# Adding up a routing matrix in DRAM by indirect scatters in place of one-hot products

## The chip, the cores and the metric

The kernel runs on one core of a Trainium2 chip. The time is device microseconds for one execution of the whole program; three runs were taken. A profile is one further execution with the hardware profiler on. Engines are named as in the profile: PE is TensorE's matrix unit, PEld its weight load, DVE VectorE, ACT ScalarE, POOL GpSimd, SP SyncE.

## The reference, cut to what matters

The program is one layer of a decoder on 512 tokens of width 1024: two mixers (a linear recurrence and a sparse attention), their gated sum and output projection, and then a PEER feed-forward layer, of which the change concerns the second half:

```
def peer_ffn(x, w_q, sub_keys, u, v):        # per block of 128 tokens; H = 8 heads, K = 16
    q = (xb @ w_q).reshape(TB, H, 2, 128)
    s = einsum('thpc,phnc->thpn', q, sub_keys)
    s1, i1 = top_k(s[:, :, 0], K);  s2, i2 = top_k(s[:, :, 1], K)
    cand = s1[..., :, None] + s2[..., None, :]       # 256 sums a head
    top_s, pos = top_k(cand, K)
    eidx = i1 * 128 + i2 at pos                      # 128 experts of 16384 for each token
    g = softmax(top_s)
    h = einsum('tkd,td->tk', u[eidx], xb)
    a = gelu(h) * g
    return einsum('tk,tkd->td', a, v[eidx])
```

## The kernel before, in words

The tokens are four blocks of 128. Block 0 is computed as the reference writes it: 128 times a row of `peer_u` is gathered for each of its tokens (`row`, L755: an indirect DMA of 128 rows of 4 KB, issued by POOL) and DVE takes a dot product with it (`u_row`, L761), then 128 times a row of `peer_v` is gathered and DVE adds it in (`v_row`, L768). Blocks 1 to 3 (`NT` = 384 tokens) are computed densely: all 16384 experts are 128 chunks of 128 experts (expert i * 128 + j is row i of chunk j). For a chunk, `u_chunk` (L739) loads 512 KB of `peer_u`, splits it into a high and a low part (ACT, DVE) and makes 24 products of 384 columns, and ACT takes gelu of the sum; `v_parts` (L883) loads 512 KB of `peer_v`, splits it likewise, multiplies the gelu with the chunk's slice of G, and `v_product` (L911) makes 18 products of 512 columns that add up in six PSUM banks until the end. G has, for each expert and token, the sum of the routing weights with which the token chose the expert: nearly all of it is zero.

The work around the change stands in this order, and a scheduler of the framework that knows what each instruction needs may set independent instructions of an engine in another order than the text has:

- Mixers, with sixteen `gate(m)` (L416), each of which stores 256 KB from a tile `t2k` (four buffers, shared with other steps) to `gate_d` through ACT's queue.
- The heads (L789): for each of 8 heads two `query`, two `scores`, some `u_chunk` (`UH`: 3 for heads 0 to 6, 7 for head 7), and `picks` (L670), the two levels of top 16 on DVE, which ends in the head's indices (`e12`, `eidx`, `iw12`). `weigh` (L713) makes the softmax of all heads after the last.
- The G stage (L806): 48 more `u_chunk`, and between them 48 groups of 8 tokens. In `g_group` DVE makes a one-hot matrix for the first index and a weighted one for the second (`oz`, `ow`), PE multiplies the two for each token (16 small products a group), ACT copies the result into `stg`, and 12 times SP stores 2 MB of it into `g_d`. `some_rows(R1)` sets one `u_row` beside each chunk but the last eight.
- The V stage (L948): chunks 76 to 127 have `u_chunk` and the v part together, then chunks 0 to 75 have the v part alone and load their gelu again from `h_d` (192 KB a chunk). Every fourth chunk loads 768 KB of G (`gj`). `R2` = 2.9 and `R3` = 0.95 rows of block 0 go beside a chunk of the one and the other kind.

`LEAD` (76) is the number of chunks whose first product is made ahead of the V stage. A row's DVE instruction is set behind the last weight split traced before it (`issue_after`). A `row` tile has four buffers. The framework puts a wait between instructions that touch the same tile or DRAM tensor.

Of the kernel before, what the change touches and what calls it, by code (L numbers as in the profile page):

```python
# [40 lines left out]
def trunk(ctx, tc, A, out, dbg=None):  # L41
# [44 lines left out]
    ya = [big.tile([P, 4, S], F32R, name="ya" + k) for k in "HL"]  # L86
    gate_d = dram.tile([16, P, S], F32, name="gate_d")
    brow_d = dram.tile([8, 640], F32, name="brow_d")
    bias_d = dram.tile([P, 8, 640], F32, name="bias_d")
# [326 lines left out]
    def gate(m):  # L416
        def evg(ps):
            g = wk.tile([P, S], F32, name="t2k", bufs=4)
            dve.tensor_tensor(g, ps, rb, op=OP.mult)
            act.activation(g, g, AF.Sigmoid)  # L420
            act.dma_start(gate_d[m], g)
        proj_T(GA + m * P, evg)

# [141 lines left out]
    gw0 = late.tile([P, P], F32, name="gw0")  # L565
    iw12 = late.tile([P, 3, 3, P], F32, name="iw12")
    NT = 3 * P
# [60 lines left out]
    act.dma_start(iota, A["iota"][:, :16])  # L628
    tva = rk.tile([P, NB, 8, 16], F32, name="tva", bufs=1)
    io16k = rk.tile([P, 16, 16], F16, name="io16k", bufs=1)  # L630
# [39 lines left out]
    def picks(h, sc2):  # L670
# [9 lines left out]
        for z in range(2):  # L680
# [5 lines left out]
                          v1[:, :, 1, None, 0:8].to_broadcast([P, NB, 15, 8]), op=OP.add)  # L686
        tv = tva[:, :, h, :]
        tp = rk.tile([P, NB, 16], U32, name="tp")
# [20 lines left out]
        dve.scalar_tensor_tensor(eidx[:, hs], e12[:, 0, 0], 128.0, e12[:, 1, 0], op0=OP.mult, op1=OP.add)  # L709
        for z in range(2):  # L710
            act.copy(iw12[:, :, z, hs], e12[:, z, 1:, :])

    def weigh():  # L713

        nm = rk.tile([P, NB, 8, 16], F32, name="nm", bufs=1)
        dve.tensor_tensor(nm, tva, tva[:, :, :, 0:1].to_broadcast([P, NB, 8, 16]), op=OP.subtract)
        act.activation(nm, nm, AF.Exp)
        ws = rk.tile([P, NB, 8], F32, name="ws")
        dve.tensor_reduce(ws, nm, axis=AX.X, op=OP.add)
        dve.reciprocal(ws, ws)  # L720
        for b in range(NB):
            o = gw0 if b == 0 else iw12[:, b - 1, 2, :]
            dve.tensor_tensor(o.rearrange("p (h k) -> p h k", h=8), nm[:, b], ws[:, b, :, None].to_broadcast([P, 8, 16]),
                              op=OP.mult)

# [3 lines left out]


    LEAD, UH, AHEAD = 76, [3] * 7 + [7], 2
    UPRE = sum(UH)
    R0, R1, R2, R3, NOROW = 0, 1, 2.9, 0.95, 8
    TG, QJ = 32, 4
    NG = NT // TG
    g_d = dram.tile([NG, P, P, TG], F32, name="g_d")
    h_d = dram.tile([LEAD, P, NT], F32, name="h_d")
# [51 lines left out]
    for h in range(8):  # L789
# [8 lines left out]
        picks(h, sc2)  # L798
    weigh()
    rks.close()  # L800
# [4 lines left out]
    vt = ctx.enter_context(tc.tile_pool(name="vt", reuse_waits="tile", bufs=2))  # L805
    with ExitStack() as st:  # L806
        gt = st.enter_context(tc.tile_pool(name="gt", reuse_waits="tile", bufs=1))
        gq = st.enter_context(tc.tile_pool(name="gq", reuse_waits="tile", bufs=2))
        gps = st.enter_context(tc.tile_pool(name="gps", reuse_waits="tile", bufs=2, space=PSUM))
        iof = gt.tile([P, P], F32, name="iof")  # L810
        act.dma_start(iof, A["iota"])

        io16 = gt.tile([P, P, 2], F16, name="io16")
        dve.tensor_copy(io16, iof[:, :, None].to_broadcast([P, P, 2]))
        TB = 8

        def g_block(b):

            ps = gps.tile([P, 512], F32, name="ps_g")
            for z in range(3):  # L820
                pe.transpose(ps[:, z * P:(z + 1) * P], iw12[:, b, z, :], ident)

            i12 = gq.tile([P, P // TB, 2, TB], F16, name="i12")
            act.copy(i12.rearrange("p g z t -> p z g t"), ps[:, :2 * P].rearrange("p (z g t) -> p z g t", z=2, t=TB))

            wt = gq.tile([P, P], F32, name="wt")
            act.activation(wt, ps[:, 2 * P:3 * P], AF.Copy, scale=16384.0)
            wp = gq.tile([P, P // TB, 2, TB], F16, name="wp")
            wg = wt.rearrange("p (g t) -> p g t", t=TB)
            act.copy(wp[:, :, 0, :], wg)  # L830
            dve.tensor_tensor(wp[:, :, 1, :], wg, wp[:, :, 0, :], op=OP.subtract)
            return i12, wp

        def g_group(b, state, t0):
            i12, wp = state
            if t0 % TG == 0:
                stgs[0] = gt.tile([P, P, TG], F32, name="stg", bufs=2)
            stg = stgs[0]
            sh = [P, TB, P, 2]

            def pairs(t):
                return t[:, t0 // TB].rearrange("p z (q two) -> p (z q) two", two=2)[:, :, None, :].to_broadcast(sh)

            oz = gq.tile(sh, F16, name="oz")
            dve.tensor_tensor(oz, io16[:, None].to_broadcast(sh), pairs(i12), op=OP.is_equal)
            ow = gq.tile(sh, F16, name="ow")
            dve.tensor_tensor(ow.rearrange("p (z q) i two -> p z (q i two)", z=2),
                              oz[:, TB // 2:].rearrange("p q i two -> p (q i two)")[:, None, :].to_broadcast(
                                  [P, 2, TB * P]), pairs(wp), op=OP.mult)
            for q in range(TB // 4):  # L850
                ps = gps.tile([P, 4, P], F32, name="ps_g")
                for k4 in range(4):
                    k = q * 4 + k4
                    for z in range(2):
                        pe.matmul(ps[:, k4, :], oz[:, k // 2, :, k % 2], ow[:, z * TB // 2 + k // 2, :, k % 2],  # L855
                                  start=(z == 0), stop=(z == 1))
                t4 = t0 % TG + q * 4
                act.copy(stg[:, :, t4:t4 + 4].rearrange("p j t -> p t j"), ps)  # L858

        stgs = [None]  # L860
        work = [(b, t0) for b in range(3) for t0 in range(0, P, TB)]
        state = {}
        done = 0
        for j in range(UPRE, LEAD):
            u_chunk(j, up.tile([P, 512], F32, name="ps_u"))
            for _ in range(len(work) * (j + 1 - UPRE) // (LEAD - UPRE) - done):
                done += 1
                b, t0 = work[done - 1]
                if t0 == 0:
                    state[b] = g_block(b)  # L870
                g_group(b, state[b], t0)
                if (t0 + TB) % TG == 0:
                    sync.dma_start(g_d[b * (P // TG) + t0 // TG], stgs[0])
            some_rows(R1 if j < LEAD - NOROW else 0)
    vs = ctx.enter_context(tc.tile_pool(name="vs", reuse_waits="tile", bufs=3))
# [4 lines left out]

    gq_t = [None]

    def v_parts(j, hgt):  # L883
# [15 lines left out]
        if j % QJ == 0:  # L899
            gq_t[0] = vs.tile([P, NG, QJ, TG], F32, name="gj", bufs=2)  # L900
            act.dma_start(gq_t[0], g_d[:, :, j:j + QJ, :].rearrange("g i j t -> i g j t"))
# [35 lines left out]

    order = list(range(LEAD, P)) + list(range(LEAD))
    vrows = list(range(P))
    ahead = [u_chunk(j, up.tile([P, 512], F32, name="ps_u")) for j in range(LEAD, LEAD + AHEAD)]  # L940
    def last_rows():
# [6 lines left out]
    for q, j in enumerate(order[:-2]):  # L948
        if LEAD + AHEAD + q < P:
            ahead.append(u_chunk(LEAD + AHEAD + q, up.tile([P, 512], F32, name="ps_u")))  # L950
        a, v = v_parts(j, ahead.pop(0) if ahead else None)
# [105 lines left out]
```

## Time and profile before

| | us |
|---|---|
| three runs: median, lowest, highest | 1711.28, 1708.59, 1711.89 |
| the profiled execution, its own time | 1711.65 |
| span of its trace, first to last instruction | 1709.9 |
| busy in the span: PE, PEld, DVE, ACT, POOL | 1675.5, 1465.9, 1340.8, 729.3, 377.0 |

A busy PE is no PE at its peak, since matmuls overlap: what one costs is the distance between the starts of two, not the length of one. Of a queue of DMA transfers the engine that issues them is busy only for the issue; a POOL instruction `DMA_INDIRECT` is the issue of an indirect transfer.

### The profile page before, as it was taken

How to read it: one execution, taken by the hardware profiler on the slowest of the kernel's cores; microseconds unless marked ns; L12 is line 12 of the kernel's file. 1: busy time of each engine (PE TensorE's matmuls, PEld its weight loads, DVE VectorE, ACT ScalarE, POOL GpSimd, SP SyncE). 2: the span in 40 equal slices, each digit the busy share in tenths (PEclk: the TensorE clock that was granted, in tenths of full speed). 3: DMA queues.
4: the chain of work that ended last, by engine and by line, in shares of the span. 5: the costliest groups of instructions: out<-in, count | busy, mean ns of one | idle time of the engine just before them, and what ended most of it. 6: DMA issues, size and time to landing. Idle time of an engine off the chain costs nothing.

```text
span 1709.9 us, 24687 instructions
## 1 busy us (share of the span) xinstructions
PE 1675.5 (98%) x9095; PEld 1465.9 (86%) x9097; DVE 1340.8 (78%) x2573; ACT 729.3 (43%) x1052; POOL 377.0 (22%) x284
## 2 busy tenths in 40 slices
PE   8999999999999999999999999999999999999997
PEld 6988887777798888999999999999999978888886
DVE  4776887547699999998988588878887888877785
ACT  4322226734443434566666433333333333333333
POOL 2000000000010000232322144444444442333320
PEclk9999999999999999999999999999999999999999
DMA  7321233127454334798988899999999999999983
GB/s 234 131 81 50 75 125 116 56 94 241 163 177 128 126 123 131 248 359 316 359 316 336 278 338 335 337 331 319 322 317 344 324 336 353 357 333 346 321 299 131
DMA packets 172472, 414.90 MB, mean 243 GB/s; under 512 B 14744, under 2 KB 85784, under 8 KB 170688
## 3 DMA queue, kind: packets, MB, share of 16 engines
q10 hardware_dynamic: 101072, 141.70, 24.4%
q1 hardware_dynamic: 34416, 137.40, 22.6%
q0 software_dynamic: 36864, 134.23, 22.4%
q8 instruction: 71, 1.16, 0.3%
q14 instruction: 49, 0.40, 0.1%
HBM read 366.86 MB, written 49.04 MB: 243 GB/s over the span
## 4 chain that ended last, share of the span: by engine, by line
PE 41%; issue 33%; DMA 11%; POOL 9%; DVE 5%; ACT 1%; POOLq 0%; SPq 0%; ACTq 0%; DVEq 0%
POOL row L757 8%; PE acc L79 6%; PE acc L77 6%; PE acc L78 6%; DMA row<-in_peer_u,eidx 5%; PE ps_mm L77 5%; PE ps_mm L79 5%; PE ps_mm L78 5%; DMA row<-in_peer_v,eidx 4%; PE ps_hg L379 2%; PE ps_hg L77 1%; PE ps_yb L460 1%; PE ps_hg L78 1%; PE ps_hg L79 1%; DMA v_raw<-in_peer_v 1%
## 5 line engine op out<-in xcount | busy, mean ns | idle before, releaser
L108 ACT CAST w_hi<-w_raw 128x1024 fp32r<-128x1024 f32 (+2 forms) x215 | 219.2, 1020 | 401.0 <-PE ps_u L78 125.4
L110 DVE TENSOR_TENSOR w_lo<-w_raw,w_hi 128x1024 fp32r<-128x1024 f32 (+2 forms) x215 | 254.9, 1185 | 84.4 <-ACT w_hi L108 72.1
L757 POOL DMA_INDIRECT row<-in_peer_u,eidx x128 | 178.5, 1394 | 553.6 <-DVE hh L762 503.6
L77 PE MATMUL ps_u<-xfH,w_hi 128*128 128x384 f32 x800 | 274.0, 343 | 1.4 <-ACT hg L744 1.4
L78 PE MATMUL ps_u<-xfL,w_hi 128*128 128x384 f32 x800 | 270.6, 338 | 0.0
L79 PE MATMUL ps_u<-xfH,w_lo 128*128 128x384 f32 x800 | 269.9, 337 | 0.0
L757 POOL DMA_INDIRECT row<-in_peer_v,eidx x128 | 178.6, 1395 | 275.5 <-DVE acc L772 253.3
L78 PE MATMUL acc<-v_lo,aH 128*128 128x512 f32 x540 | 211.2, 391 | 3.3 <-DVE v_lo L895 3.3
L77 PE MATMUL acc<-v_hi,aH 128*128 128x512 f32 x540 | 212.1, 393 | 1.4 <-ACT aH L906 1.1
L79 PE MATMUL acc<-v_hi,aL 128*128 128x512 f32 x540 | 212.1, 393 | 0.1
L906 ACT CAST aH<-aj 128x384 fp32r<-128x384 f32 x128 | 65.6, 513 | 308.7 <-DVE aj L903 138.1
L772 DVE SCALAR_TENSOR_TENSOR acc<-row,ah,acc 128x1024 f32<-128x1024 f32 x127 | 162.6, 1281 | 21.4 <-DMA row<-in_peer_v,eidx 20.7
L762 DVE CUSTOM_DVE_ANT_0 scr<-row,xf 128x1024 f32<-128x1024 f32 x128 | 156.3, 1221 | 20.1 <-DMA row<-in_peer_u,eidx 19.3
L77 PEld LDWEIGHTS ps_u<-xfH,w_hi 128*128 128x128 f32 x800 | 150.2, 188 | 3.5 <-ACT hg L744 1.7
L78 PEld LDWEIGHTS ps_u<-xfL,w_hi 128*128 128x128 f32 x800 | 150.5, 188 | 2.2
L79 PEld LDWEIGHTS ps_u<-xfH,w_lo 128*128 128x128 f32 x800 | 150.2, 188 | 0.0
L895 DVE TENSOR_TENSOR v_lo<-v_raw,v_hi 128x1024 fp32r<-128x1024 f32 x90 | 110.0, 1223 | 24.1 <-ACT v_hi L894 23.5
L78 PEld LDWEIGHTS acc<-v_lo,aH 128*128 128x128 f32 x540 | 101.7, 188 | 24.0 <-DVE v_lo L895 3.6
L79 PEld LDWEIGHTS acc<-v_hi,aL 128*128 128x128 f32 x540 | 101.8, 188 | 23.2 <-DVE aL L908 0.8
L77 PEld LDWEIGHTS acc<-v_hi,aH 128*128 128x128 f32 x540 | 101.7, 188 | 22.1 <-ACT aH L906 1.4
L894 ACT CAST v_hi<-v_raw 128x1024 fp32r<-128x1024 f32 x90 | 94.4, 1048 | 51.6 <-PE acc L79 19.9
L858 ACT COPY stg<-ps_g 128x512 f32<-128x512 f32 x96 | 99.6, 1158 | 3.3 <-PE ps_g L855 3.3
(313 smaller groups left out, 3367.4 us busy)
## 6 DMA issues: line engine op xcount, KB each, us to landing
w_raw<-in_uT SPq DMA_DIRECT2D x128, 512.0 KB
v_raw<-in_peer_v ACTq DMA_DIRECT2D x90, 512.0 KB
g_d<-stg SPq DMA_DIRECT2D x12, 2048.0 KB
gj<-g_d ACTq DMA_DIRECT2D x32, 768.0 KB
w_raw<-in_peer_v ACTq DMA_DIRECT2D x38, 512.0 KB
w_raw<-in_wT SPq DMA_DIRECT2D x31, 512.0 KB
h_d<-hg ACTq DMA_DIRECT2D x76, 192.0 KB
hgr<-h_d ACTq DMA_DIRECT2D x76, 192.0 KB
```

The lines of the kernel that those rows point to most:

```text
L77: pe.matmul(ps, lh, rh, start=first, stop=False, **kw)
L78: pe.matmul(ps, lh, rl, start=False, stop=False, **kw)
L79: pe.matmul(ps, ll, rh, start=False, stop=last, **kw)
L108: act.copy(hi[:, :n], raw[:, :n])
L110: pace[0] = dve.tensor_tensor(lo[:, :n], raw[:, :n], hi[:, :n].bitcast(F32), op=OP.subtract)
L757: pool.indirect_dma_start(out=g, out_offset=None, in_=A[tab], in_offset=bass.IndirectOffsetOnAxis(ap=eidx[:, k:k + 1], axis=0))
L762: dve.tensor_tensor_reduce(out=scr, in0=row("peer_u", k), in1=xf0, scale=1.0, scalar=0.0, op0=OP.mult, op1=OP.add, accum_out=hh[:, k:k + 1])
L772: dve.scalar_tensor_tensor(acc, row("peer_v", k), ah[:, k:k + 1], acc, op0=OP.mult, op1=OP.add)
L858: act.copy(stg[:, :, t4:t4 + 4].rearrange("p j t -> p t j"), ps)
L894: act.copy(vh, raw)
L895: pace[0] = dve.tensor_tensor(vl, raw, vh.bitcast(F32), op=OP.subtract)
L906: act.copy(aH, gj)
```

## The change

G is one DRAM tensor for each block (`g_d[0..2]`, 16384 experts by 128 tokens, 8 MB each). Beside gates 0 to 5 ACT's queue fills them with zeros (12 transfers of 2 MB). `picks` makes, for each head, the softmax weights at once (in place of `weigh`) and the address of each weight (`gi`, expert * 128 + token), and then issues 48 indirect scatters through POOL: for each k of 16 and each block of 3, 128 weights (one a partition, 4 bytes) are added to the words of `g_d[b]` that `gi` names. `gi` and `wh`, which a scatter reads, have three buffers, one a head. The one-hot stage goes. `LEAD` is 96: 32 chunks in the heads (4 a head), 64 between the heads and the V stage, 32 in the V stage with both parts, 96 with the v part alone. Rows of block 0 go beside them at rates 0, 0.7, 2.7 and 1.4. The G of four chunks is loaded one group ahead, as three transfers of 256 KB.

```
+    g_d = [dram.tile([P * P, P], F32, name="g_d%d" % b) for b in range(3)]
+    nil = consts.tile([P, 512], F32, name="nil")
+    pool.memset(nil, 0.0)
...
             act.dma_start(gate_d[m], g)
+            if m < 6:
+                for z in range(2):
+                    act.dma_start(g_d[m // 2][(m % 2 * 2 + z) * 32 * P:(m % 2 * 2 + z + 1) * 32 * P, :].rearrange(
+                        "(p r q) t -> p r (q t)", p=P, q=4), nil[:, None, :].to_broadcast([P, 8, 512]))
...
-        for z in range(2):
-            act.copy(iw12[:, :, z, hs], e12[:, z, 1:, :])
-    def weigh():
...
+        ef = rk.tile([P, 3, 16], F32, name="ef")
+        dve.scalar_tensor_tensor(ef, e12[:, 0, 1:], 128.0, e12[:, 1, 1:], op0=OP.mult, op1=OP.add)
+        gi = rk.tile([P, 3, 16], I32, name="gi", bufs=3)
+        dve.tensor_scalar(gi, ef, 128.0, pcol, op0=OP.mult, op1=OP.add)
+        nm = rk.tile([P, NB, 16], F32, name="nm")
+        dve.tensor_tensor(nm, tv, tv[:, :, 0:1].to_broadcast([P, NB, 16]), op=OP.subtract)
         act.activation(nm, nm, AF.Exp)
+        ws = rk.tile([P, NB], F32, name="ws")
         dve.tensor_reduce(ws, nm, axis=AX.X, op=OP.add)
         dve.reciprocal(ws, ws)
+        wh = rk.tile([P, 3, 16], F32, name="wh", bufs=3)
+        dve.tensor_tensor(wh, nm[:, 1:], ws[:, 1:, None].to_broadcast([P, 3, 16]), op=OP.mult)
+        dve.tensor_scalar(gw0[:, hs], nm[:, 0], ws[:, 0:1], None, op0=OP.mult)
+        for k in range(16):
+            for b in range(3):
+                pool.indirect_dma_start(out=g_d[b].rearrange("e (t one) -> (e t) one", one=1),
+                                        out_offset=bass.IndirectOffsetOnAxis(ap=gi[:, b, k:k + 1], axis=0),
+                                        in_=wh[:, b, k:k + 1], in_offset=None, compute_op=OP.add)
...
-    LEAD, UH, AHEAD = 76, [3] * 7 + [7], 2
+    LEAD, UH, AHEAD = 96, [4] * 8, 2
-    R0, R1, R2, R3, NOROW = 0, 1, 2.9, 0.95, 8
+    R0, R1, R2, R3 = 0, 0.7, 2.7, 1.4
...
-    with ExitStack() as st:
...
+    for j in range(UPRE, LEAD):
+        u_chunk(j, up.tile([P, 512], F32, name="ps_u"))
+        some_rows(R1)
...
+    def g_load(q):
+        if q < P and q % QJ == 0:
+            gqs[q] = vs.tile([P, 3, QJ, P], F32, name="gj", bufs=2)
+            for b in range(3):
+                act.dma_start(gqs[q][:, b], g_d[b].rearrange("(i j) t -> i j t", j=P)[:, order[q]:order[q] + QJ, :])
...
-        dve.scalar_tensor_tensor(gj.rearrange("p (g t) -> p g t", t=TG), gq_t[0][:, :, j % QJ, :], 1.0 / 16384,
-                                 hgt.rearrange("p (g t) -> p g t", t=TG), op0=OP.mult, op1=OP.mult)
+        dve.tensor_tensor(gj.rearrange("p (b t) -> p b t", b=3), gq_t[0][:, :, j % QJ, :],
+                          hgt.rearrange("p (b t) -> p b t", b=3), op=OP.mult)
```

## Rows read from the trace of the kernel before

**Rows 1.** Busy time by stage (heads, G stage, V stage both parts, v alone).

```profile
core 0: us, PE busy (x) PEld busy (x) DVE busy (x) ACT busy (x) POOL busy (x), PEclk, DMA share, GB/s
460.00:691.00 231.00, 224.12 (x1221) 203.06 (x1219) 215.59 (x941) 97.27 (x143) 5.04 (x6) 1.00 0.42 136
691.00:955.00 264.00, 261.05 (x1988) 252.84 (x1989) 220.85 (x238) 170.55 (x207) 71.05 (x45) 1.00 0.88 322
963.00:1374.00 411.00, 410.19 (x2057) 372.56 (x2058) 333.51 (x424) 144.60 (x199) 188.47 (x140) 1.00 0.93 327
1374.00:1690.00 316.00, 312.40 (x1349) 253.90 (x1348) 251.36 (x308) 113.12 (x157) 93.64 (x69) 0.99 0.94 325
```

**Rows 2.** PE in order of time: a u chunk's products, then a v chunk's.

```profile
472.37 0.34 PE L79 MATMUL ps_hg<-xfH,w_lo 128*128 128x384 f32 x1
472.55 0.34 PE L77 MATMUL ps_hg<-xfH,w_hi 128*128 128x384 f32 x1
...
1600.64 0.39 PE L79 MATMUL acc<-w_hi,aL 128*128 128x512 f32 x1
1600.87 0.39 PE L77 MATMUL acc<-w_hi,aH 128*128 128x512 f32 x1
```

**Rows 3.** Gelus of u chunks (L744) counted in the G stage.

```profile
700.00:950.00 250.00, 22.81 (x48) 1.00 0.88 323
```

**Rows 4.** Costliest groups by line: mean ns of one, idle before, releaser.

```profile
L757 POOL DMA_INDIRECT row<-in_peer_v,eidx x128 | 178.6, 1395 | 275.5 <-DVE acc L772 253.3 <-issue 10.3 <-DVE hh L762 5.6
L858 ACT COPY stg<-ps_g 128x512 f32<-128x512 f32 x96 | 99.6, 1158 | 3.3 <-PE ps_g L855 3.3
L845 DVE TENSOR_TENSOR oz<-io,i 128x2048 f16<-128x2048 f16 x48 | 58.5, 1219 | 0.0
L855 PE MATMUL ps_g<-ow,oz 128*128 128x128 f16 x768 | 52.8, 219 | 2.4 <-ACT stg L858 2.4
```

**Rows 5.** POOL in order of time: start, length, gap before it.

```profile
502.34 0.94 POOL L757 DMA_INDIRECT row<-in_peer_u,eidx  x1 [0.30 <-issue]
503.59 0.94 POOL L757 DMA_INDIRECT row<-in_peer_u,eidx  x1 [0.30 <-issue]
...
1119.38 1.34 POOL L757 DMA_INDIRECT row<-in_peer_u,eidx  x1 [0.30 <-issue]
1121.02 1.31 POOL L757 DMA_INDIRECT row<-in_peer_u,eidx  x1 [0.30 <-issue]
...
1127.64 1.71 POOL L757 DMA_INDIRECT row<-in_peer_u,eidx  x1 [0.30 <-issue]
```

**Rows 6.** Index writes of the 8 heads on DVE (L709).

```profile
L709 DVE SCALAR_TENSOR_TENSOR eidx<-e x8: 166/174/175, 498.2 to 688.1; 128x16 int32<-128x16 f32 x8
```

**Rows 7.** A store to DRAM (L203), and a transfer that reads it (L205).

```profile
L203 ACTq DMA_DIRECT2D brow_d<-brow x1: 522/522/522, 25.7 to 25.7; - x1
...
L205 ACTq DMA_DIRECT2D bias_d<-brow_d x1: 564/564/564, 28.2 to 28.2; - x1
```

**Rows 8.** The chain that ended last, 990 to 1020 us: start, length.

```profile
997.06 8.22 DMA row<-in_peer_u,eidx
```

**Rows 9.** Loads of G (L901) and the product that takes one (L903).

```profile
L901 ACTq DMA_DIRECT2D gj<-g_d x32: 367/384/659, 955.2 to 1669.9; - x32
...
L903 DVE SCALAR_TENSOR_TENSOR aj<-gj,hg x52: 548/552/559, 962.7 to 1374.2; 128x384 f32<-128x384 f32 x52
```

**Rows 10.** Gates 0 to 5, then the rest: ACT busy (x), clock, DMA share, GB/s.

```profile
195.00:250.00 55.00, 3.81 (x6) 1.00 0.26 86
250.00:327.00 77.00, 16.58 (x18) 1.00 0.35 112
```

**Rows 11.** The stretch with most DMA, columns as in rows 1.

```profile
1400.00:1500.00 100.00, 99.92 (x434) 81.17 (x433) 85.07 (x104) 37.95 (x52) 30.47 (x25) 1.00 1.01 356
```

More of the change, by code (lines that the diff above doesn't have):

```diff
@@ L565, in trunk @@
     gw0 = late.tile([P, P], F32, name="gw0")
-    iw12 = late.tile([P, 3, 3, P], F32, name="iw12")
+    pcol = late.tile([P, 1], F32, name="pcol")
     NT = 3 * P
@@ L628, in trunk @@
     act.dma_start(iota, A["iota"][:, :16])
-    tva = rk.tile([P, NB, 8, 16], F32, name="tva", bufs=1)
+    act.dma_start(pcol, bass.AP(tensor=A["iota"].tensor, offset=A["iota"].offset, ap=[[1, P], [1, 1]]))
     io16k = rk.tile([P, 16, 16], F16, name="io16k", bufs=1)
@@ L686, in picks @@
                           v1[:, :, 1, None, 0:8].to_broadcast([P, NB, 15, 8]), op=OP.add)
-        tv = tva[:, :, h, :]
+        tv = rk.tile([P, NB, 16], F32, name="tv")
         tp = rk.tile([P, NB, 16], U32, name="tp")
@@ L709, in picks @@
         dve.scalar_tensor_tensor(eidx[:, hs], e12[:, 0, 0], 128.0, e12[:, 1, 0], op0=OP.mult, op1=OP.add)
-        for z in range(2):
-            act.copy(iw12[:, :, z, hs], e12[:, z, 1:, :])
-    def weigh():
-        nm = rk.tile([P, NB, 8, 16], F32, name="nm", bufs=1)
-        dve.tensor_tensor(nm, tva, tva[:, :, :, 0:1].to_broadcast([P, NB, 8, 16]), op=OP.subtract)
+        ef = rk.tile([P, 3, 16], F32, name="ef")
[4 more added lines that the diff above has]
+        dve.tensor_tensor(nm, tv, tv[:, :, 0:1].to_broadcast([P, NB, 16]), op=OP.subtract)
         act.activation(nm, nm, AF.Exp)
-        ws = rk.tile([P, NB, 8], F32, name="ws")
+        ws = rk.tile([P, NB], F32, name="ws")
         dve.tensor_reduce(ws, nm, axis=AX.X, op=OP.add)
         dve.reciprocal(ws, ws)
[L721 to L724, printed above, removed]
-    LEAD, UH, AHEAD = 76, [3] * 7 + [7], 2
+        wh = rk.tile([P, 3, 16], F32, name="wh", bufs=3)
[7 more added lines that the diff above has]
+    LEAD, UH, AHEAD = 96, [4] * 8, 2
     UPRE = sum(UH)
-    R0, R1, R2, R3, NOROW = 0, 1, 2.9, 0.95, 8
-    TG, QJ = 32, 4
-    NG = NT // TG
-    g_d = dram.tile([NG, P, P, TG], F32, name="g_d")
+    R0, R1, R2, R3 = 0, 0.7, 2.7, 1.4
+    QJ = 4
     h_d = dram.tile([LEAD, P, NT], F32, name="h_d")
@@ L798, in trunk @@
         picks(h, sc2)
-    weigh()
     rks.close()
@@ L805, in trunk @@
     vt = ctx.enter_context(tc.tile_pool(name="vt", reuse_waits="tile", bufs=2))
-    with ExitStack() as st:
[L807 to L874, printed above, removed]
@@ L879, in trunk @@
     v3 = A["peer_v"].rearrange("(i j) d -> i j d", j=P)
-    gq_t = [None]
+    order = list(range(LEAD, P)) + list(range(LEAD))
+    gqs, gq_t = {}, [None]
+    def g_load(q):
[3 more added lines that the diff above has]
+                act.dma_start(gqs[q][:, b], g_d[b].rearrange("(i j) t -> i j t", j=P)[:, order[q]:order[q] + QJ, :])
     def v_parts(j, hgt):
@@ L898, in v_parts @@
             act.dma_start(hgt, h_d[j])
-        if j % QJ == 0:
-            gq_t[0] = vs.tile([P, NG, QJ, TG], F32, name="gj", bufs=2)
-            act.dma_start(gq_t[0], g_d[:, :, j:j + QJ, :].rearrange("g i j t -> i g j t"))
         gj = vs.tile([P, NT], F32, name="aj")
-        dve.scalar_tensor_tensor(gj.rearrange("p (g t) -> p g t", t=TG), gq_t[0][:, :, j % QJ, :], 1.0 / 16384,
-                                 hgt.rearrange("p (g t) -> p g t", t=TG), op0=OP.mult, op1=OP.mult)
+        dve.tensor_tensor(gj.rearrange("p (b t) -> p b t", b=3), gq_t[0][:, :, j % QJ, :],
+                          hgt.rearrange("p (b t) -> p b t", b=3), op=OP.mult)
         aH = vs.tile([P, NT], F32R, name="aH")
@@ L936, in finish, with take @@
             q.dma_start(out[b * P:(b + 1) * P, n * 512:(n + 1) * 512], g[:, n, :])
-    order = list(range(LEAD, P)) + list(range(LEAD))
     vrows = list(range(P))
+    g_load(0)
+    def take(q):
+        if q % QJ == 0:
+            gq_t[0] = gqs.pop(q)
+            g_load(q + QJ)
+        return order[q]
     ahead = [u_chunk(j, up.tile([P, 512], F32, name="ps_u")) for j in range(LEAD, LEAD + AHEAD)]
@@ L950, in trunk @@
             ahead.append(u_chunk(LEAD + AHEAD + q, up.tile([P, 512], F32, name="ps_u")))
+        take(q)
         a, v = v_parts(j, ahead.pop(0) if ahead else None)
```

## The prediction

> **What bounds the kernel now.** I read the time by stage first: in every stage PE is busy for all but a few us, at a granted clock of 0.99 to 1.00, with DVE below it and DMA at a share of 0.42 in the heads but 0.88 to 0.94 after them [rows 1]. Since matmuls overlap, I priced them by the distance of two starts in PE's order of time: 0.176 us for 384 columns and 0.23 us for 512 [rows 2]. A u chunk is then 24 × 0.176 = 4.2 us, a v chunk 18 × 0.23 = 4.1 us, both together 8.3 us. The G stage runs 48 chunks in 250 us [rows 3], 5.2 us a chunk: forming G costs PE 1.0 us a chunk, 47 us in all. PE bounds every stage, but DMA is close: at its busiest it moved 356 GB/s at a share of 1.01 [rows 11].
>
> **What goes.** With the one-hot groups go 47 us of PE, and on DVE and ACT work that did not bound: 48 × 2 DVE instructions of about 1.22 us and 96 ACT copies of 1.16 us [rows 4]. The u chunks that change place keep their price, so with nothing late the span would be 1709.9 − 47 = 1663 us. The first v product now comes some 8 us after the first load of G is issued [rows 9], at about 963 us; with 20 more u chunks ahead of it and no G products PE would be ready for it at 963 − 47 + 20 × 4.2 = 1000 us. From it to the end are 1663 − 1000 = 663 us of PE.
>
> **What the heads get.** Four u chunks instead of three a head is 4.2 us more PE beside 1.2 us for the weight split on DVE and seven small DVE instructions in place of `weigh`. DVE is at 216 of 231 us there and PE at 224 [rows 1], so PE, which gets more, stays the bound, and this is in the count above.
>
> **The scatters.** 384 indirect transfers all go through POOL, which has almost nothing to do in the heads. No scatter stands in this trace; the nearest row is the gather, which also takes 128 addresses. Its issue takes 0.94 us and the next starts 0.30 us later when DVE does not disturb it, so at least 1.24 us each; back to back in the V stage it takes 1.31, 1.34 and 1.71 [rows 5], and the mean of all rows of `peer_v` is 1.395 [rows 4], 1.70 with the gap. DVE is less busy with large two-operand work between the heads and the V stage than there. I take 1.45 us, and keep 1.24 and 1.70 for the range (a scatter that is cheaper than a gather is a rival below).
>
> Head 0 has its indices at 498.2 us [rows 6]; with the weights behind them the first scatter can start at about 502. A head makes 48 × 1.45 = 70 us of scatters, but a head lasts only (231 + 4 × 4.2) / 8 = 31 us [rows 1], so POOL falls behind at once and never waits for work again. The last scatter ends at 502 + 384 × 1.45 = 1059 us (978 at 1.24, 1155 at 1.70).
>
> Do their waits add to that? Each scatter writes the tensor that the third scatter before it wrote, so it waits for that one to land. The nearest wait on a store to DRAM is 2.5 us from the store's issue to that of the transfer which reads it, at light load [rows 7]; three issues are 3 × 1.45 = 4.35 us, so the wait is covered. Under load a gather takes 8.2 us from issue to landing, most of it 512 KB of data and other traffic [rows 8]; were a scatter to take that, the wait would bound. I take it as covered, nearer to the small store, and make the other a rival.
>
> *A page on that wait.* The Trainium skill, "DMA: Bandwidth & Descriptors", section "Rules for kernel authors", says that an accumulating transfer reads its destination and writes it later, that another write in between is lost, and that one has to wait for the earlier one's semaphore. No row here shows this.
>
> **Who waits.** `g_load(0)` reads all three tensors, so no v product starts before the last scatter has landed: 1059 + 8 = 1067 us, 67 us after PE could. Behind the scatters on POOL stand the row gathers; DVE's `u_row` waits for them, and behind `u_row` stand the weight splits that PE waits for. `gi` and `wh` have three buffers, so head 7's must wait until head 4's scatters have landed, at 502 + 5 × 70 = 852 us, and DVE, which runs in order, can stand there with splits behind it. Both stalls fall before the V stage and into the same 67 us: the chain on POOL sets the end either way.
>
> **The V stage as a transfer problem.** PE needs 663 us for it. The bytes: u 30 × 0.524 MB, v 128 × 0.524, G 25.2, gelus 96 × 0.197, output 2.1, which is 129 MB; rows 256 × 0.524 = 134 MB if POOL had no time for them earlier. 263 MB at 356 GB/s are 739 us. If 45 rows get between the scatters, the V stage has 239.5 MB, 673 us, but POOL ends 45 × 1.45 = 65 us later: 739 + 1067 = 1806 against 673 + 1132 = 1805. So 1806 both ways. If DMA can give 397 GB/s, the stage is 663 us (this end goes into the range); G's load in runs of 2 KB instead of 512 bytes may help a little.
>
> **The zeros.** 25.2 MB go out on ACT's queue in the 55 us of gates 0 to 5, where 86 GB/s are used [rows 10]: at 356 − 86 = 270 GB/s 14.9 MB fit, and the other 10.3 MB, at 356 − 112 = 244, last 42 us longer. Weights come on SP's queue and have share to spare, but `gate_d`'s stores stand behind the zeros on ACT's queue, and each holds one of four `t2k` buffers, which later gates and `select` need. Between nothing and 42 us, I take 15, and since it comes before head 0 it moves everything: 1806 + 15 = 1821 us of span. What lies around the span is 1711.65 − 1709.9 = 1.75 us, and the profiled execution stood 0.4 us above the median, so 1821 + 1.75 − 0.4: about 1822 us.
>
> **The rivals.**
>
> *Scatters keep up.* POOL's issue of a scatter is much cheaper than that of a gather, so the last lands before 1000 us. Then PE sets the pace: 1663 + 0 to 15 = 1663 to 1678; with the transfers' 673 us in the V stage up to 1690. For it: a scatter moves 4 bytes, not 4 KB, per address. Against: a gather's 0.94 us is POOL's own time, in which no data moves. It decides where the V stage's start and the transfers give back the 47 us: with 739 us of V stage below (1711 − 739 − 8 − 15 − 502) / 384 = 1.16 us a scatter, with 663 us below 1.36 us. That is the span of the doubt: a rate near 1.24 with a DMA near 397 GB/s would also land here, at 978 + 8 + 15 + 663 = 1664, or 1678 with PE's 1000.
>
> The Trainium skill speaks for this rival: "DMA: Bandwidth & Descriptors", section "Anatomy of one DMA — SWDGE (gpsimd) path", puts the fixed 2.0 us of a DMA from this path mostly down to the receipt of the write and calls making descriptors small. By that, three chains of 128 would take 128 × 2.0 = 256 us, an estimate from that page, and the scatters would be free. The gathers' rows disagree on the issue: 0.94 us and more of POOL each [rows 5].
>
> *Each scatter waits for a landing.* Under load a round of three takes 6 us, between the 2.5 us of the small store and the 8.2 us of the gather [rows 7, 8]: 502 + 128 × 6 = 1270, + 8 + 15 + 739 = 2032 us. It decides when a landing takes longer than 4.35 us. For it: the share of DMA is 0.88 and more after the heads now. Against: between heads and V stage there is 512 + 192 KB a chunk of 4.2 us, and a row now and then, far from full.
>
> *It does nothing measurable.* Late scatters cost just the 47 us that PE gains; within 0.2%, which is about what a measurement of this kernel can tell from no change.
>
> **The numbers.** The forecast, POOL's issue as the bound, has 0.60, and by its own bounds goes from 978 + 8 + 739 = 1725 to 1155 + 8 + 739 + 42 = 1944 us. Scatters keep up: 0.20 (1663 to 1707). Landing bound: 0.15 (about 2032, from 1900 up). Nothing measurable: 0.05. So faster 0.20, the same 0.05, slower 0.75. The range has to leave out 2 in 10: I take 1680 to 1940, which cuts half of the keep-up case and most of the landing case, 0.10 each.
>
> **What would show it.** Right: POOL is busy without a gap from about 505 until past 1050 us, PE has a hole of some 50 to 100 us ahead of its first v product, DVE's waits ahead of `u_row` or `gi` name POOL or DMA, DMA is at 350 GB/s or more for most of the V stage, and v chunks alone come every 4.6 us or so instead of 4.1. Wrong: the first v product at about 1000 us with PE unbroken (keep-up), or gaps on POOL of over 1 us between scatters that name a DMA (landing bound). For the zeros: idle time in 200 to 320 us that names `gate_d`. What would make the number wrong most easily is the price of one scatter: 0.1 us is 38 us at the end.

## The result, and the profile after

The changed kernel takes 2141.09 us (median of 4 runs, 2139.67 to 2145.05) against 1710.01 us before (4 runs, 1708.59 to 1711.89): 1.2517 times as long, 95% interval 1.2488 to 1.2546. Slower was forecast, but with 1822 us; the time is 319 us above that and outside the range.

Busy time in stretches of the kernel after; the first two are the stretches of the heads and of the G stage in [rows 1], the third ends as the last scatter is issued, and the last two are the V stage, with both parts and with the v part alone:

```profile
core 0: us, PE busy (x) PEld busy (x) DVE busy (x) ACT busy (x) POOL busy (x), PEclk, DMA share, GB/s
460.00:691.00 231.00, 178.83 (x954) 161.00 (x952) 147.93 (x622) 84.06 (x112) 151.97 (x94) 0.90 0.48 110
691.00:955.00 264.00, 92.83 (x472) 85.55 (x472) 83.82 (x371) 44.48 (x57) 221.44 (x138) 0.69 0.35 47
...
1200.00:1300.00 100.00, 42.16 (x186) 40.55 (x185) 12.99 (x16) 8.62 (x12) 83.54 (x55) 0.70 0.50 97
...
1440.00:1694.00 254.00, 254.00 (x1282) 231.70 (x1281) 198.56 (x285) 91.55 (x125) 114.12 (x78) 1.00 0.89 310
1694.00:2139.00 445.00, 414.82 (x1761) 331.91 (x1759) 368.37 (x441) 151.95 (x211) 172.71 (x128) 0.98 0.92 342
```

Where PE was busy for 261 of 264 us before [rows 1] it is busy for 93 now, and POOL for 221. PE's granted clock is 0.69 there, a mean between its two levels; it is back at 1.00 as the V stage begins. The page draws the same in 40 slices of 53 us, in tenths: POOL's plateau runs from about 510 to 1300 us, and PE's hole lies inside it, from about 640 us, where DVE first stands long at `wh`, until the last scatter.

```profile
PE   8999999999982606225555636999999999999987
...
POOL 1000000003888888888888883123445454454330
PEclk9999999999996858567877867999999999999999
```

What POOL does in the plateau, by line and then in order of time; these answer to the gathers of [rows 4, 5]:

```profile
L737 POOL DMA_INDIRECT g_d<-wh,gi x384 | 634.4, 1652 | 119.6 <-issue 114.6 <-DMA g_d<-wh,gi 4.9
```

```profile
999.74 2.01 POOL L737 DMA_INDIRECT g_d<-wh,gi  x1 [0.30 <-issue]
1002.05 1.56 POOL L737 DMA_INDIRECT g_d<-wh,gi  x1 [0.30 <-issue]
1003.91 2.05 POOL L737 DMA_INDIRECT g_d<-wh,gi  x1 [0.30 <-issue]
```

The issue of a scatter takes 1.65 us in the mean, not the 0.94 of an undisturbed gather or the 1.395 that those of `peer_v` took in the mean [rows 4], and with the gap 1.65 + 119.6 / 384 = 1.96 us. The gap is the same 0.30 us. Waits for a landing are 4.9 us in all 384, so the landing is covered.

First and last start of the scatters, of G's loads (answering to [rows 9]), of the zeros, of the first kind of v product and of `aH`, each from the view of one tile's instructions:

```profile
L737 POOL DMA_INDIRECT g_d<-wh,gi x384: 1552/1558/2597, 514.0 to 1300.3; - x192
L834 ACTq DMA_DIRECT2D gj<-g_d x96: 325/443/1385, 1298.4 to 2085.6; - x96
L429 ACTq DMA_DIRECT2D g_d<-nil x12: 520/521/699, 22.1 to 141.8; - x12
...
L77 PE MATMUL acc<-v_hi,aH x480: 387/389/632, 1446.9 to 2125.7; 128*128 128x512 f32 x160
...
L856 ACT CAST aH<-aj x128: 502/514/520, 1440.6 to 2117.5; 128x384 fp32r<-128x384 f32 x128
```

The V stage (counted from the first `aH` at 1441 us, 140 us after the last scatter) takes 699 us. Why it didn't start at 1302 + 8 = 1310 us is in the waits (us in total, times, longest):

```profile
DVE wh L732 <- DMA g_d<-wh,gi: 259.3, 5, 62.8
DVE scr L774 <- DMA row<-in_peer_u,eidx: 208.1, 26, 16.7
...
PE ps_hg L79 <- DVE w_lo L114: 179.4, 4, 58.8
PE ps_u L79 <- DVE w_lo L114: 179.0, 22, 61.1
...
ACT hg L756 <- DMA g_d<-wh,gi: 60.6, 1, 60.6
...
DVE aj L853 <- DMA hgr<-h_d: 54.0, 36, 3.5
```

DVE stands 259 us for a buffer of `wh`, in five of the eight heads, since the scatters of an earlier head have not read it yet, and 208 us for rows, which POOL gathers between scatters. The weight splits behind these in DVE's order come late, and PE waits for them, 358 us in the heads and after. So when the last scatter lands, 34 u chunks are still to do, at 4.2 us each 143 us.

### The profile page after: what moved, and what is told of

Read it like the earlier page. It is cut to its first block, busy times and chain, and to the rows that moved or that the text cites. A ratio compares the mean times of both kernels' runs of the same rounds, so it can differ in the third digit from the quotient of the medians.

```text
span 2139.5 us, 23585 instructions
## 1 busy us (share of the span) xinstructions
PE 1680.3 (79%) x8320; PEld 1461.0 (68%) x8320; DVE 1234.0 (58%) x2522; ACT 652.2 (30%) x952; POOL 995.4 (47%) x669
## 3 DMA queue, kind: packets, MB, share of 16 engines
q0 software_dynamic: 92160, 134.46, 25.6%
## 4 chain that ended last, share of the span: by engine, by line
PE 34%; POOL 30%; issue 13%; DMA 13%; DVE 7%; ACT 2%; ACTq 1%; SPq 0%; POOLq 0%; DVEq 0%
POOL g_d L737 27%; DMA hgr<-h_d 4%; PE ps_mm L77 4%; PE ps_mm L79 4%; PE ps_mm L78 4%; PE acc L79 4%; PE acc L78 4%; PE acc L77 4%; DMA w_raw<-in_peer_v 3%; DMA g_d<-wh,gi 2%; PE ps_u L79 2%; PE ps_u L77 2%; PE ps_u L78 2%; POOL row L769 2%; DMA v_raw<-in_peer_v 2%
## 5 line engine op out<-in xcount | busy, mean ns | idle before, releaser
L737 POOL DMA_INDIRECT g_d<-wh,gi x384 | 634.4, 1652 | 119.6 <-issue 114.6
L79 PE MATMUL ps_u<-xfH,w_lo 128*128 128x384 f32 x768 | 275.2, 358 | 179.0 <-DVE w_lo L114 179.0
L769 POOL DMA_INDIRECT row<-in_peer_u,eidx x128 | 165.2, 1290 | 291.2 <-DVE hh L774 228.1
L79 PE MATMUL ps_hg<-xfH,w_lo 128*128 128x384 f32 x256 | 89.4, 349 | 179.4 <-DVE w_lo L114 179.4
L79 PE MATMUL acc<-v_hi,aL 128*128 128x512 f32 x480 | 189.0, 394 | 2.0 <-DVE aL L858 1.8
L78 PE MATMUL acc<-v_lo,aH 128*128 128x512 f32 x480 | 188.0, 392 | 2.8 <-DVE v_lo L848 2.8
L77 PE MATMUL acc<-v_hi,aH 128*128 128x512 f32 x480 | 188.1, 392 | 0.0
L71 POOL TENSOR_TENSOR rs_r<-rs_ms,half 128x1 f32<-128x1 f32 (+1 forms) x13 | 11.2, 864 | 357.8 <-DVE rs_ms L69 357.8
L79 PEld LDWEIGHTS ps_hg<-xfH,w_lo 128*128 128x128 f32 x256 | 50.1, 196 | 180.7 <-DVE w_lo L114 180.7
L79 PE MATMUL acc<-w_hi,aL 128*128 128x512 f32 x288 | 115.6, 401 | 10.8 <-DVE aL L858 10.8
```

The source lines that it names most:

```text
L71: pool.tensor_tensor(r, ms, half[:, :k], op=OP.pow)
L77: pe.matmul(ps, lh, rh, start=first, stop=False, **kw)
L78: pe.matmul(ps, lh, rl, start=False, stop=False, **kw)
L79: pe.matmul(ps, ll, rh, start=False, stop=last, **kw)
L737: pool.indirect_dma_start(out=g_d[b].rearrange("e (t one) -> (e t) one", one=1), out_offset=bass.IndirectOffsetOnAxis(ap=gi[:, b, k:k + 1] ...
L769: pool.indirect_dma_start(out=g, out_offset=None, in_=A[tab], in_offset=bass.IndirectOffsetOnAxis(ap=eidx[:, k:k + 1], axis=0))
```

## The experiments

Each is one run beside one of the kernel before on the same chip, which took 1703 to 1714 us; the last two have 6 and 12 runs, beside 17 of the kernel before. Single runs carry no interval, so no reading below rests on a difference of a few us. V start is the start of the first `aH`.

**Eight buffers for the scatters' operands**, so that no head waits for an earlier head's scatters.

```
-        gi = rk.tile([P, 3, 16], I32, name="gi", bufs=3)
+        gi = rk.tile([P, 3, 16], I32, name="gi", bufs=8)
-        wh = rk.tile([P, 3, 16], F32, name="wh", bufs=3)
+        wh = rk.tile([P, 3, 16], F32, name="wh", bufs=8)
```

> gi and wh get eight buffers each, one for every head, so no DVE instruction has to wait for a scatter; nothing else changes. Theory 'price and buffers' (a scatter holds POOL for 1.65 + 0.30 = 1.95 us, and the waits of wh for scatters, 259 us on DVE, kept PE from its u chunks): the first v product comes some 8 us after the last scatter, at about 1310 us instead of 1441, and the time falls by about 130 us to 2010. Rival 'rows take over' (u_row's gathers stand behind the scatters on POOL, and DVE then stands at u_row in place of wh): the time stays within 30 us of 2141 and DVE's waits for gathered rows grow from 208 us to 400 or more.

2140.04 us, V start at 1436: no gain. The heads are done by 740 us, but then DVE meets `u_row`, whose gather stands behind the scatters. The wait and a stretch of this run:

```profile
DVE scr L774 <- DMA row<-in_peer_u,eidx: 451.5, 26, 251.9
```

```profile
800.00:1000.00 200.00, 0.00 (x0) 0.00 (x0) 0.00 (x0) 0.00 (x0) 167.34 (x108) 0.50 0.23 0
```

The 208 us of waits for rows became 452; for 200 us nothing but POOL runs, with PE's granted clock at its lower level. The rows took over from the buffers.

**The rows out of the way as well**: none between the heads and the V stage, more in it.

```
 (gi and wh as above)
-    R0, R1, R2, R3 = 0, 0.7, 2.7, 1.4
+    R0, R1, R2, R3 = 0, 0, 4, 1.45
```

> Eight buffers as in the run before it, and no row of block 0 is set beside the u chunks ahead of the V stage (rates 0, 0, 4 and 1.45 in place of 0, 0.7, 2.7 and 1.4). Price and buffers: POOL has 384 scatters alone, the last ends at about 514 + 384 x 1.95 = 1263 us; the V stage then has all 256 rows, 263 MB, 711 to 739 us: 1980 to 2010 us, like the run before it. Rows take over: this run is 100 us or more faster than the run before it, since only here DVE has nothing left to stand at.

2191.41 us, which neither expected, and V start at 1437 again. DVE no longer stands for `wh`, its waits for rows have fallen to 70 us, and a third gate shows, here in the waits and in ACT's order of time:

```profile
ACT hg L756 <- DMA g_d<-wh,gi: 406.3, 1, 406.3
```

```profile
872.39 0.33 ACTq L758 DMA_DIRECT2D h_d<-hg  x1
1274.58 3.96 ACTq L834 DMA_DIRECT2D gj<-g_d  x3
1278.64 0.49 ACT L756 ACTIVATE hg<-ps_u 128x384 f32<-128x384 f32 x1 [406.29 <-DMA g_d<-wh,gi]
```

The first load of G is issued by ACT, at a place in its order at which 39 of the 98 u chunks ahead of the V stage are still to come, and waits there for the last scatter; all of ACT's gelus and splits wait behind it. In the changed kernel the same wait shows as 61 us, since ACT came to that place only at 1242 us, held up by what DVE owed it. This run is 51 us longer than the one before because its V stage, with all late rows, takes 752 us.

**That load issued by POOL**, which at that place has nothing but scatters ahead.

```
 (as the run before)
-                act.dma_start(gqs[q][:, b], g_d[b]...
+                (pool if q < 8 else act).dma_start(gqs[q][:, b], g_d[b]...
```

> As the second experiment (eight buffers for gi and wh, the row gathers late), and the first two loads of G are issued by POOL instead of ACT. Theory (three in-order queues hold work behind a scatter: DVE at gi and wh, DVE at u_row, ACT at the load of G; with none of them left, POOL alone sets the start of the V stage): ACT has no wait of more than 20 us ahead of a gelu, the 96 u chunks and the two ahead are done by about 1040 us as in the run without scatters, the last scatter comes at about 1275 us as before, the first aH at 1275 + 8 = 1283 us instead of 1437, and with 700 to 750 us of V stage the time is 1985 to 2040 us instead of 2191. Rival (the V stage starts at 1437 because of something else that the last scatter releases, and the three gates are only where it shows): the first aH stays near 1437 us and the time near 2190 us.

2043.87 us, just past the end of what was expected. 97 of the 98 gelus are out before the last scatter, which ends at 1295; V start follows at 1301. What waits now is a v part, for G itself (first the start of `aH`, from the view of its line):

```profile
L856 ACT CAST aH<-aj x128: 503/513/519, 1301.3 to 2022.8; 128x384 fp32r<-128x384 f32 x128
...
DVE aj L853 <- DMA gj<-g_d: 265.8, 1, 265.8
```

Undoing the three gates is worth 97 us: the V stage starts 139 us earlier, but has nearly all rows to take and lasts 741 us, 42 more.

**No scatters** (G stays zero: blocks 1 to 3 get no routed output).

```
-        for k in range(16):
+        for k in range(0):
```

> No scatter is issued (G stays zero: the sum over the experts of blocks 1 to 3 is left out of the result); zeros, weights, addresses, loads of G and all products stay. The prediction's count of the rest: the span before less 47 us of PE, plus 11 us that the zeros cost ahead of the heads, and a V stage between 663 us (PE) and 699 us (as measured after): 1675 to 1712 us. If the V stage is still at 699 us here, with 45 rows set before it, it is the transfers of the 96 v chunks alone that cost the 36 us; if it is at 663, they came from rows that the scatters had pushed into it.

1716.35 us, a little over the 1675 to 1712 expected, where the kernel before took 1702.57 on that chip. V start is at 1012 us, against a forecast of 1000 plus the zeros. The V stage takes 703 us though the rows come on time, in two stretches (both parts, then v alone):

```profile
1012.00:1264.00 252.00, 252.00 (x1271) 229.80 (x1270) 196.52 (x281) 90.46 (x125) 114.23 (x78) 1.00 0.88 310
1264.00:1714.00 450.00, 419.87 (x1763) 335.12 (x1762) 370.66 (x443) 152.26 (x211) 174.84 (x129) 0.97 0.92 339
```

PE needs 96 × 4.14 = 397 us for the 96 v chunks alone and gets through them in 450, of which some 9 follow the last product. So with this `LEAD` and these row rates, scatters that cost nothing would not have beaten the kernel before.

**No scatters, and 76 chunks ahead as before** (with the row rates of before; G zero again).

```
-    LEAD, UH, AHEAD = 96, [4] * 8, 2
+    LEAD, UH, AHEAD = 76, [3] * 7 + [7], 2
-    R0, R1, R2, R3 = 0, 0.7, 2.7, 1.4
+    R0, R1, R2, R3 = 0, 1, 2.9, 0.95
```

> No scatter is issued, so G stays zero and blocks 1 to 3 get no routed output; and 76 chunks have their first product ahead, with the row rates of the kernel before, instead of 96. Theory (in the run without scatters the V stage takes 40 us more than PE needs because the 20 more spilled gelus and the rows bring it to the limit of the transfers): the first aH at about 1012 - 20 x 4.2 = 928 us, the V stage is bound by PE at about 747 us, and the time is 1675 to 1690 us, below the kernel before. Rival (the V stage's rate is set by something else, such as the new load of G): 1705 to 1725 us, as in the run with 96 chunks.

1662.65 us, better than either expected: 51 us below the kernel before, zeros included. The stretch with both parts and the one with the v part alone:

```profile
912.00:1325.00 413.00, 413.00 (x2084) 376.77 (x2083) 339.64 (x418) 146.68 (x201) 204.14 (x141) 1.00 0.92 328
1325.00:1660.00 335.00, 327.29 (x1423) 266.75 (x1421) 253.60 (x321) 123.34 (x174) 71.90 (x64) 1.00 0.84 300
```

PE is busy in 740 of these 748 us. The time falls by 51 us although the zeros stay, which come to some 12 us (below), so what went with the one-hot stage is worth some 60 us here and not 47. 20 more chunks ahead (with rates to suit) cost all of the gain again: 1716 against 1663, though on a chip on which the kernel before was 11 us faster.

**Scatters that write without adding** (two heads of a token that chose one expert keep one of two weights), in the changed kernel as it is.

```
-                                        in_=wh[:, b, k:k + 1], in_offset=None, compute_op=OP.add)
+                                        in_=wh[:, b, k:k + 1], in_offset=None)
```

> The scatters write the weights and do not add them (the add is left out, so an expert that two heads choose for one token keeps one of the two weights); number, addresses and waits are the same. If the add is what makes a scatter dear for POOL, its issue falls from 1.56 us undisturbed to the 0.94 to 1.0 us of a gather, the last scatter ends at about 514 + 384 x 1.35 + 23 x 1.35 = 1064 us, and the time falls to about 1064 + 8 + 700 = 1770 to 1830 us. If it is the scatter into DRAM or its 4 byte elements, the issue stays at 1.5 us or more and the time within 30 us of 2141.

2041.09 us, far over the 1770 to 1830 expected for a cheaper scatter. The scatters by line:

```profile
L737 POOL DMA_INDIRECT g_d<-wh,gi x384 | 396.9, 1034 | 200.1 <-issue 116.5 <-DVE gi L723 61.7 <-DMA g_d<-wh,gi 21.8
```

1.03 us against 1.65 (medians 0.97 and 1.56): the adding is what makes a scatter dearer to POOL than a gather. But the last scatter came at 1201, not at 514 + 384 × 1.33 = 1025 us, since the heads were late; so the price could not be read from the end.

**The same on the kernel without the three gates.**

> As the run with the loads of G issued by POOL, and the scatters write without adding (two heads of a token that chose one expert keep one of the two weights). In the first run without the add the heads themselves were late, so the price of the add could not be read from the end. Theory (with no in-order queue behind the scatters, their price on POOL alone sets the start of the V stage): 384 x (1.03 + 0.31) us from 514 put the last scatter at about 1030 us in place of 1293, the V stage starts at about 1040 and takes 740 to 760 us, so 1780 to 1805 us, 240 to 265 us less than with the add. Rival (without the add the landing becomes the bound, three scatters to one landing of more than 4 us): POOL waits for scatters' DMA for over 50 us and the time stays over 1850 us.

2143.74 us, neither theory's. The scatters cost 1.01 us, without waits for landings (4.0 us in all), but the heads took until 1084 us. In stretches of them in which the scatters come 1.28 us apart, PE goes through a u chunk like this:

```profile
639.99 0.48 PE L77 MATMUL ps_hg<-xfH,w_hi 128*128 128x384 f32 x1 [2.32 <-issue]
642.79 0.48 PE L78 MATMUL ps_hg<-xfL,w_hi 128*128 128x384 f32 x1 [2.32 <-issue]
645.59 0.48 PE L79 MATMUL ps_hg<-xfH,w_lo 128*128 128x384 f32 x1 [2.32 <-issue]
```

2.8 us a product where it took 0.176 [rows 2], and no releaser that the trace knows.

**And with a filler on POOL**: a tile is set to zero after each scatter, so that they come further apart.

```
 (as the run before)
+                pool.memset(pad, 0.0)
```

> As the run before it (scatters that write without adding, loads of G issued by POOL), and POOL sets a tile of 128x512 to zero after each scatter, 0.53 us, so that scatters come every 1.85 us or so, near the 1.95 us of those with the add, and not every 1.28. In the two runs without the add PE's products in the heads came 1.4 to 2.8 us apart in stretches in which it waited for nothing that the profile names, with DVE and ACT slow beside it. Theory (the rate is what slows the other engines: scatters 1.28 us apart take something that all engines need): PE's products in the heads are 0.18 us apart again, all heads are done by about 770 us, and the time is that of the run with the add and the same loads, 2000 to 2050 us. Rival (it is the write without the add itself, at any rate): PE's waits for nothing named stay over 100 us in the heads, and the time is 2150 us or more.

1914.95 us, below the 2000 to 2050 expected. The scheduler set over half of the fillers ahead of the heads, so that scatters are 1.68 us apart in the mean, 1.84 in the heads (as a rule three at 1.28 us and then a pause with two fillers) and 1.27 at the end, after PE's u chunks. PE in the same place:

```profile
640.00 0.34 PE L79 MATMUL ps_hg<-xfH,w_lo 128*128 128x384 f32 x1
640.18 0.34 PE L77 MATMUL ps_hg<-xfH,w_hi 128*128 128x384 f32 x1
640.35 0.34 PE L78 MATMUL ps_hg<-xfL,w_hi 128*128 128x384 f32 x1
```

The stall is gone, though the scatters still do not add: it belongs to plain scatters that follow each other without a pause, not to the plain write as such. Whether the mean rate or the pause decides was not separated. And this gives the price of POOL's time: against the run with the add and the same loads, the distance of two scatters falls from 2.03 to 1.68 us, 384 times 136 us; V start falls by 132 us and the time by 129.

**Half of the scatters**, without the three gates (G lacks the 8 smaller weights of each head).

```
-        for k in range(16):
+        for k in range(8):
```

> As the run with the loads issued by POOL, but only the first 8 of the 16 weights of a head are scattered (192 scatters in place of 384; G lacks the 8 smaller weights of each head). Theory (POOL's time for the scatters sets the start of the V stage once the other gates are gone): the last scatter comes at about 514 + 192 x 1.95 = 890 us, before PE has its u chunks done, so the V stage starts at about 1012 to 1040 us and the time is 1715 to 1770 us, still not below the kernel before; against the full run some 250 us for 192 scatters. Rival (the gates cost what they cost whatever the number of scatters): the time stays over 1900 us.

1786.46 us, 257 below the full number. The last ends at 924 us and V start is at 1036, set by PE. The time is 16 us over the upper end of what was expected; the V stage, with all late rows, took 749 us. Half of the work is still slower than the kernel before.

**One DRAM tensor for the three blocks**, so that each scatter waits for the one before it.

```
-    g_d = [dram.tile([P * P, P], F32, name="g_d%d" % b) for b in range(3)]
+    g_all = dram.tile([3 * P * P, P], F32, name="g_all")
 (gi with the block's first word added; without the three gates)
```

> As the run before it, but the three blocks of G lie in one DRAM tensor, so that each scatter waits for the one just before it and not for the third before it. Theory (a landing takes 2 to 4 us and is covered by three issues, so that it has cost nothing so far): the distance of two scatters grows from 1.95 us to one landing and one issue, about 3.5 to 4.5 us, POOL's waits name the scatter's DMA, the last scatter comes at 514 + 384 x 3.5 to 4.5 = 1860 to 2240 us and the time is 2570 to 3000 us. Rival (the 1.95 us are already a landing's wait that the profile books as issue): the distance stays below 2.5 us and the time below 2200 us.

2654.32 us; two scatters are 3.63 us apart in the mean. In order of time, with what the gap ahead of each waits for:

```profile
1302.27 1.56 POOL L741 DMA_INDIRECT g_all<-wh,gi  x1 [1.82 <-DMA g_all<-wh,gi]
1305.40 1.56 POOL L741 DMA_INDIRECT g_all<-wh,gi  x1 [1.58 <-DMA g_all<-wh,gi]
1308.67 1.56 POOL L741 DMA_INDIRECT g_all<-wh,gi  x1 [1.71 <-DMA g_all<-wh,gi]
```

A landing is some 3.3 us after the start of the issue, below three issues of 1.96: that is why the changed kernel hardly waits for one.

**An attempt to beat both**: the kernel before, with one block of three by scatters (eight buffers, a third of the zeros) and two by one-hot products, and the rows eight chunks later; beside it the later rows alone.

```
+    g_s = dram.tile([P * P, P], F32, name="g_s")
...
+        for k in range(16):
+            pool.indirect_dma_start(out=g_s..., in_=wh[:, k:k + 1], in_offset=None, compute_op=OP.add)
...
-        work = [(b, t0) for b in range(3) for t0 in range(0, P, TB)]
+        work = [(b, t0) for b in (1, 2) for t0 in range(0, P, TB)]
-            some_rows(R1 if j < LEAD - NOROW else 0)
+            some_rows(R1 if UPRE + NOROW <= j else 0)
```

> The kernel before (76 chunks ahead, one-hot products) with one of the three blocks of G added up by scatters: 16 scatters a head in place of 48, eight buffers for gi and wh, one third of the zeros, and the rows of peer_u start eight chunks after the heads, so that no DVE instruction stands behind a scatter. Theory (a scatter costs 1.6 to 1.95 us of POOL and nothing else as long as no in-order queue stands behind it): a head lasts about 28 us and takes 16 x 1.6 to 1.95 = 26 to 31 us of scatters, so POOL keeps pace and is done by 515 + 128 x 1.95 = 765 us at the latest, long before the first load of G; PE loses a third of the one-hot products, 16 us, and gains 4 us of zeros: 1711 - 16 + 4 = 1699 us, 1687 if the 12 us by which the run without scatters fell below its sum come here too. Rival (the scatters cost other engines something in the heads, or the second load and multiplication of G in the V stage does): 1711 us or more.

> The kernel before, and only the rows of peer_u start eight chunks after the heads and run to the end of that stage, where before they start at once and pause for the last eight chunks. It separates what the run beside it gains by the scatters from what it gains by the place of the rows. Theory: within 0.3 per cent of the kernel before. Rival: this alone makes the difference.

1927.45 us, 1.1273 times the kernel before (1.1241 to 1.1305); the later rows alone 1.005 (1.0031 to 1.0069), a little over what was expected. My expectation for the first was wrong by its own evidence: one block is one tensor, and the run with one tensor had shown what that does.

```profile
765.87 1.56 POOL L734 DMA_INDIRECT g_s<-wh,gi  x1 [1.71 <-DMA g_s<-wh,gi]
769.23 1.55 POOL L734 DMA_INDIRECT g_s<-wh,gi  x1 [1.80 <-DMA g_s<-wh,gi]
```

The 128 scatters took until 1047 us, 4.2 us each, with rows behind them on POOL, for which DVE stood 229 us in all (the longest wait 120). No version that I tried beats the kernel before with a right G.

## Why the prediction was wrong

*What held.* POOL's time for the scatters is the main chain: PE has a hole, DVE's waits name the rows and `wh`, POOL hardly waits for a landing. In the V stage PE is no longer the bound at 96 chunks: the stage takes 699 us where PE needs 663, and v chunks alone come every 445 / 96 = 4.6 us, as forecast. That this is the transfers is supported, not shown: their share is 0.92 in that stretch, and DVE waits 54 us for gelus coming back, but DVE itself is busy for 368 of the 445 us.

*What came out near by luck.* The zeros were to go out beside gates 0 to 5, from 195 us, and hold up `t2k` buffers. The scheduler set all twelve between 22 and 142 us. There, from 50 to 150 us, the transfers' share is 0.86 in place of 0.23 and PE is busy for 93 us in place of 100; the first gate is stored at 211 us instead of 200, and head 0 has its indices at 511 instead of 498. So they cost 11 to 13 us of the 15 taken, at another place and not through `gate_d`, for which the engines wait 3 us in all. The sum for PE's first v product, 1000 us and the zeros, meets the 1012 measured without scatters because two misses cancel: with 76 chunks ahead the same sum gives 963 - 47 + 12 = 928 and the run had 912, so what went with the one-hot stage cost more than 47 us; with 96 ahead PE stood for some 12 us in the heads (busy for 221 of 233), which the forecast had left unbroken.

*The step that failed first: the price of a scatter.* I took 1.45 us from the gather, with 1.70 as the upper bound. It is 1.96: 0.51 × 384 = 196 us. What a gather doesn't have is the add; without it the issue takes 0.97 us again, as cheap as a gather. The bounds came from rows of one kind of operation and could not hold a part that this kind lacks. The first scatter came at 514 us (502 and 15 forecast), and 26 row gathers between the scatters made them later by some 35 us.

*The V stage.* It was 40 us shorter than the 739 taken, but not by the forecast's exchange ("1806 both ways"): 54 rows were gathered ahead of it, half of them in the 140 us after the last scatter, and by 263 MB less 54 × 0.524 MB at 356 GB/s, 660 us, PE's 663 should have been the bound. The stage moved 330 GB/s in the mean: while both parts run PE is busy throughout and the transfers stay at 310, and with the v part alone they reach 342. One sum over the whole stage hides that its two stretches have different bounds.

*The step that failed second:* "Both stalls fall before the V stage and into the same 67 us: the chain on POOL sets the end either way." They did not, since work that has to be done before or in the V stage stood behind them. The forecast needed PE to have its u chunks behind it when the last scatter lands; it had 34 left, and V start was at 1441 us and not at 1310. That is 131 us. With the price the terms add up to what was missing: 196 + 131 + 35 (rows) - 3 (first scatter) - 40 (V stage) = 319 us. The experiments name three gates in a row, each hidden by the one before: `wh`'s three buffers and the rows (both on DVE, both in the forecast, as harmless), and the load of G in ACT's queue, which I had not seen. With all three gone, POOL does set the V start, and the forecast's own form gives the time: 514 + 384 × 2.03 + 8 + 739 = 2041 us of span against 2042. The 2.03 us is that run's own distance of two scatters, so this tests the form and not the price; and 739 against 741 us of V stage is near by luck, since 339 GB/s were moved, not 356.

*The rivals.* "Landing bound" came nearest in size (2032), for a reason that was not there. "Scatters keep up" would not have given 1663 to 1707 us at this `LEAD`, but 1716: more chunks ahead move products out of the stretch that PE bounds and into one that something else bounds. Beside a v chunk alone stand 0.524 MB of `peer_v`, 0.197 of G, 0.197 of gelu and 1.4 rows, 1.65 MB, which in PE's 4.14 us would be 399 GB/s; at the 0.95 rows of the run with 76 chunks it is 342. So the transfers are the likely bound (an estimate), but `LEAD` was not tested apart from the rates of the rows, and rows are also DVE's work.

The Trainium skill's "DMA: Bandwidth & Descriptors", section "Anatomy of one DMA — SWDGE (gpsimd) path", from which "Scatters keep up" was also drawn, calls making descriptors small and puts a fixed 2.0 us mostly down to the landing; the traces put 1.56 us of a scatter with an add on POOL, and some 1.7 us of landing behind it.

*Open:* why scatters without an add, 1.28 us apart, slow PE, DVE and ACT. It went away when fillers stood between them in the heads; what they take from the other engines was not found. Why the add costs POOL 0.6 us more was not found either. Where 76 or 96 chunks with fewer scatters might gain was not tried further.

## What to carry to other kernels

Price an operation that the trace doesn't have with its every part: an accumulating scatter is no gather, and half a microsecond, 384 times, was 196 us. A late producer is only a bound on the end if nothing else queues up behind its consumers: for each in-order engine ask what stands behind the first instruction that waits, its DMA issues too, and expect the next gate when one is removed. Before moving work ahead of a bound stage, look at whether the stage that gets the rest is still bound by the same thing.

## What the runs showed of the hardware

- An indirect scatter of 128 words of 4 bytes holds POOL for 0.97 us when it writes and 1.56 us when it adds (medians), with a gap of 0.30 us behind either. Of the 384 with an add in the changed kernel 69 took over 1.65 us, up to 2.6; 63 of these ran beside a DVE instruction of over 1 us that reads two operands, and 43 of the other 315.
- A scatter with an add has landed about 3.3 us after its issue began (run with one tensor).
- A scatter makes 144 packets when it adds and 32 when it writes: the page counts 92160 packets on POOL's DMA queue with the adds, 49152 without the add and 36864 with no scatters. Where nothing else ran, adding scatters 1.86 us apart kept the DMA engines busy for a share of 0.23 (run with eight buffers, 840 to 960 us) and plain ones 1.27 us apart for 0.02 (run with the filler, 1050 to 1150 us).
- Plain scatters 1.28 us apart stretched PE's products from 0.18 to as much as 2.8 us, at a DMA share of 0.14 to 0.18; at 1.84 us apart in the mean, with pauses, they did not.
- Transfers reached 386 GB/s in a slice of the V stage, over the 356 [rows 11] that I had taken as their most.
